# Moving rows 144 bytes from the weights in place of 64, modulo 256, in a decoder step on one Trainium2 core

## The chip, the core and the metric

The kernel runs on one core of one Trainium2 chip. The metric is device time in microseconds (us) of one execution, the median of several runs. The core has TensorE (PE: matrix products; its weight loads are listed apart as PEld), VectorE (DVE), ScalarE (ACT), GpSimd (POOL) and SyncE (SP), which issues the transfers between the large memory and the core's own memory, SBUF. SBUF has 128 partitions; a tensor in it takes the same range of bytes in each of its partitions, and this range is what "address" means below. A matrix product takes 128 x 128 weights, which a weight load brings into TensorE, and streams "moving rows" against them: 128 partitions of, for example, 288 float32 columns.

## What is computed

One step of one layer of a decoder with two kinds of head, RWKV-7 and retention, on 16 meta tokens, a prompt of 256 tokens and 8 x 4 sampled tokens (304 tokens in all), with width 2048:

```python
xn = rms_norm(x, norm_mix)
z = xn @ w_in                                   # 2048 -> 3360 + 4096 columns
o_a, S_a = rwkv7_mixer(z[..., :RWKV_COLS], ...) # 16 heads of 64
o_b, S_b = retention_mixer(z[..., RWKV_COLS:], ...)  # 4 heads of 256
h = x + concatenate([o_a, o_b]) @ w_out
hn = rms_norm(h, norm_ffn)
h = h + (silu(hn @ w_gate) * (hn @ w_up)) @ w_down   # 2048 -> 5632 -> 2048
y = rms_norm(h, norm_final)
```

Outputs are `y` without the meta tokens, the last projected row for the token shift, and both kinds of state.

## The kernel before

**Products in three passes.** All large products are float32 in value, but run as one-pass products on a rounded type (`float32r`). Each weight tile and each row is split into a high part (`wh`, `xh`) and the rest (`wl`, `xl`), and a tile product is the sum of three: `wh` x `xh`, `wh` x `xl`, `wl` x `xh` (lines 719 to 721). The small products of the mixers run on plain float32 and are not one-pass.

**The main loop** (`main`, lines 683 to 726) walks through a fixed list of weight tiles: first the input projection (`in`, 16 steps of 128 rows for each tile of 128 output columns), then the output projection in two halves of 8 steps (`out`), then the feed-forward part (`gate`, `up`, and `down` in groups of 4 steps). Weights come as 128 x 512 pieces: `wr` is filled by a transfer (`load`), ScalarE rounds it into `wh`, VectorE subtracts into `wl` (`cast` and `rest`); five buffers each.

**Columns of the moving rows.** A job says which columns of a row it streams (`cols`). Most input jobs stream all 304 (`T`). Those of the r part, and the second and third of the first three, start at column 14 (290 columns). Those of the retention gates and of q start at column 16 (288 columns). Output and feed-forward jobs work without the meta tokens and stream columns 0 to 288 (`TO`). A column is 4 bytes, so a job that starts at column 16 reads from an address 64 bytes further on than one that starts at column 0.

**Where things lie.** `xh` and `xl` are tiles of 16 rows of `XW` = 320 columns (1280 bytes, five times 256), so all 16 rows have one address modulo 256. They are the first tiles of the pool `cp`, followed by `pv`, `ones`, `omu`, `cst`, `shout` and `half`. Behind this pool lie `wr`, `wh` and `wl` (2048 bytes each), and then two arenas, one of float32 and one of float32r, in which all other tiles have places that a planner found. The down products' rows (`act`, two rows of `XW` for each tile) lie in the float32r arena; `GAP` columns at the end of the float32 arena set where that one begins.

**Order.** The order of all instructions is worked out ahead in a draft of the program, from operations and sizes, and then kept. `half` holds four sets of eight scalars for each partition, written once by four VectorE operations and read by ScalarE as bias and scale in each of the eight pairs of heads (`pair`, lines 1001 to 1010); `omu` holds scalars of the token shift.

Of the kernel before, what the change touches and what calls it, by code (L numbers as in the profile page):

```python
# [8 lines left out]
F32 = mybir.dt.float32  # L9
F32R = mybir.dt.float32r  # L10
# [5 lines left out]
P = 128  # L16
D = 2048
KT = D // P
# [4 lines left out]
T = META + SEQ + NB * NS  # L23
XW = T + 16
TO = SEQ + NB * NS
# [51 lines left out]
KEYS = ((0, META, SEQ, 0), (P, P, NP - P, SEQ), (LASTK, 2 * P, T - 2 * P, SEQ + NP - P))  # L77
RMW = SEQ + NP - P + T - 2 * P
ROOM = 33040
GAP = 56  # L80
WIDE = 4200
FREE, GAPS, TRIES = 800.0, (2000.0, 1000.0, 500.0, 200.0, 50.0, 0.0), 12

# [120 lines left out]
def pack(x_prompt, x_sample, state_shift, state_rwkv, state_ret, meta_tokens, norm_mix, w_in,  # L204
# [55 lines left out]
    r = r.reshape(NB // 2, 2, RH, 2, P, RD)  # L260
    out["s0r"] = ca(r.transpose(2, 0, 4, 3, 1, 5))
    c, rm, cs, _ = constants()
    out["cst"], out["rmask"], out["cs"] = c, rm, ca(cs)
    return out
# [34 lines left out]
class Timed:  # L299


    def __init__(self, plan, eng, name):
        self._plan, self._eng, self._name = plan, eng, name
# [280 lines left out]
class Step:  # L584


    def __init__(self, tc, I, O, ctx, rooms, draft, log):
        self.tc, self.nc, self.I, self.O = tc, tc.nc, I, O
        self.rooms, self.draft = rooms, draft
        pool = lambda n, b, **k: ctx.enter_context(tc.tile_pool(name=n, bufs=b, **k))  # L590
        self.cp = pool("const", 1)
        self.wp = pool("weights", 1)
        self.mp = pool("scratch", 1)
        self.ap_ = pool("acc", ACC, space=bass.MemoryType.PSUM)
        self.pp = pool("psum", 8 - ACC, space=bass.MemoryType.PSUM)
        self.n, self.tags = 0, {}
        self.plan = pl = Plan(self.nc, rooms, draft, log, (lambda i: i) if draft else tc.keep_in_program_order)
        self.sp = pl.sp
        if not draft:
            self.arena = {dt: self.mp.tile([P, r.size + (GAP if dt == F32 else 0)], dt, tag=f"arena_{dt}", name=f"arena_{dt}")  # L600
                          for dt, r in rooms.items()}
        self.pe, self.dve, self.act, self.pool = pl.pe, pl.dve, pl.act, pl.pool
        pl.outside = {v.name for v in (*I.values(), *O.values())}
        self.outs = []
        self.live = 0
        self.done = set()
# [182 lines left out]
    def start(self):  # L789
        I = self.I  # L790
        self.pvt = self.t([P, NPV], "pv", pool=self.cp)
        self.ones = self.t([P, P], "ones", pool=self.cp)
        self.dve.memset(self.ones, 1.0)

        self.omu = self.t([P, 46], "omu", pool=self.cp)
        self.eps = {}
        for c, e in enumerate((RMS_EPS, GN_EPS, 4 * RMS_EPS), 27):
            self.eps[e] = self.omu[:, c:c + 1]
            self.pool.memset(self.eps[e], e)
        xh, xl = self.xh, self.xl  # L800
        warm = self.t([P, 1], "warm")
        self.act.activation(warm, self.ones[:, :1], AF.Tanh)

        gx = self.t([P, KT + KT * T], "xr")
        self.gx = gx[:, :KT]
        xr = self.xr = gx[:, KT:].rearrange("p (k t) -> p k t", t=T)
        x = lambda a, b: self.sp.dma_start(xr[:, a:b], xT(I)[:, a:b, :])
        self.sp.dma_start(gx[:, :KT + T], I["xT"][:, :KT + T])
        self.load(2)
        x(1, 2)  # L810
        self.load(2)
        self.sp.dma_start(self.pvt, I["pv"])
        x(2, 3)
        self.load(2)
        x(3, 4)
        self.load(2)
        for k in range(4, KT, 2):
            self.load()
            x(k, k + 2)
        self.converted = 0  # L820

        pt = self.ps()
        for _ in range(WARM):
            self.pe.matmul(pt[:, :P], self.ones, self.ones, start=True, stop=True)
# [12 lines left out]
    def constants(self):  # L837

        I, xr = self.I, self.xr
        self.csr = self.t([P, 2, T], "csr")  # L840
        self.sp.dma_start(self.csr, I["cs"])
        self.shin = self.t([P, 27, NB], "shin")
        self.sp.dma_start(self.shin, I["shift"])
        self.cst = self.t([P, NCV], "cst", pool=self.cp)
        self.sp.dma_start(self.cst, I["cst"])
        for g in range(0, KT, 4):
            self.act.activation(xr[:, g:g + 4], xr[:, g:g + 4], AF.Square)
            if g % 8:
                self.dve.tensor_add(xr[:, g - 4:g], xr[:, g - 4:g], xr[:, g:g + 4])
            yield  # L850
        for a, n in (8, 4), (2, 2), (1, 1):
            self.dve.tensor_add(xr[:, :n], xr[:, :n], xr[:, a:a + n])
        yield
        yield
        ssq = self.ps()
        self.pe.matmul(ssq[:, :T], self.ones, xr[:, 0, :], start=True, stop=True)
        self.rstd1 = self.t([P, T], "rstd")
        yield
        yield from self.rsqrt(ssq[:, :T], 1.0 / D, RMS_EPS, out=self.rstd1)
        self.dve.tensor_mul(self.csr, self.csr, self.rstd1[:, None, :].to_broadcast([P, 2, T]))  # L860
        self.shout = self.t([P, 27, 9], "shout", pool=self.cp)
        self.pool.memset(self.shout, 0.0)

        self.half = self.t([P, 4, 8], "half", pool=self.cp)
        for i, n in enumerate(("w0", "a0", "ka")):
            self.dve.tensor_scalar(self.half[:, i, :], self.pvt[:, PV[n]:PV[n] + 8], 0.5, None, op0=ALU.mult)
        self.dve.tensor_scalar(self.half[:, 3, :], self.pvt[:, PV["ka"]:PV["ka"] + 8], -0.5, 1.0,
                               op0=ALU.mult, op1=ALU.add)
        self.dve.tensor_scalar(self.omu[:, :27], self.pvt[:, :27], -1.0, 1.0, op0=ALU.mult, op1=ALU.add)
        self.done.add("const")  # L870
# [848 lines left out]
    def ffn_jobs(self):  # L1719
        dve, act = self.dve, self.act  # L1720
        hold = {}

        def gu_post(f, f0, up, acts, last):
            def g(acc):
                t = self.t([P, TO], "fu" if up else "fg")
                dve.tensor_mul(t, acc[:, :TO], self.rstd2)
                yield
                if not up:
                    act.activation(t, t, AF.Silu)
                    hold[f] = t  # L1730
                    return
                while f not in hold:
                    yield
                dve.tensor_mul(t, t, hold.pop(f))
                yield
                hl = self.t([P, 2, XW], "act", F32R)[:, :, :TO]
                act.copy(hl[:, 0, :], t)
                yield
                dve.tensor_sub(hl[:, 1, :], t, hl[:, 0, :])
                acts[f - f0] = hl[:, 0, :], hl[:, 1, :]  # L1740
                if last:
                    self.done.add(("act", f))
            return g
# [51 lines left out]
    def build(self, gam4):  # L1795
        self.gam4 = gam4
        self.shifts = 0
        self.os, self.on, self.gates, self.ht, self.xs_of = [None] * KT, {}, {}, [], {}
        self.xh = self.t([P, KT, XW], "xh", F32R, pool=self.cp)[:, :, :T]
        self.xl = self.t([P, KT, XW], "xl", F32R, pool=self.cp)[:, :, :T]  # L1800
        self.xs = [(self.xh[:, k, :], self.xl[:, k, :]) for k in range(KT)]
        jobs = [self.z_job(i, self.lora_post(i), c0=META - 2 if i else 0) for i in range(3)]
        for h in range(NPAIR):
            jobs += self.pair_jobs(h)
        for h in range(RH):
            jobs += self.ret_jobs(h) + self.gate_jobs(h)
        jobs += self.out_jobs(0) + self.out_jobs(1) + self.ffn_jobs()
        jobs = {j.key: j for j in jobs}
        self.raws, self.halves, self.rests, self.loaded, self.halved = [], [], [], 0, 0
        self.start()  # L1810
        self.plan.run(self.main(jobs))
        self.flush(all=True)
# [5 lines left out]
def xT(I):  # L1818

    return I["xT"][:, KT:].rearrange("p (k t) -> p k t", t=T)  # L1820
# [19 lines left out]
def body(tc, I, O):  # L1840
    from contextlib import ExitStack
    gam4 = constants()[3]
    rooms = {F32: Room(), F32R: Room()}
    nc = draft(I, O)
    log = []
    Step(tile.TileContext(nc[0]).__enter__(), nc[1], nc[2], ExitStack(), rooms, True, log).build(gam4)
    rooms[F32R].place(WIDE)
    rooms[F32].place(ROOM - rooms[F32R].size)
    with ExitStack() as ctx:
        Step(tc, I, O, ctx, rooms, False, log).build(gam4)  # L1850
# [22 lines left out]
```

## Time and profile before

| what | value |
|---|---|
| median of 3 runs | 1545.88 us (1543.72 to 1546.4) |
| span of the profiled execution | 1544.2 us, the only time of it that is shown |
| busy, TensorE products | 1527.5 us, 99% of the span |
| busy, weight loads | 1499.9 us, 97% |
| busy, VectorE | 1089.4 us, 71% |
| busy, ScalarE | 866.5 us, 56% |
| mean granted clock of TensorE | 0.996 |

The profile was taken in one execution. Busy time of TensorE counts from the start of an instruction to its modelled end, and neighbouring products overlap, so the mean duration of a product (near 295 ns) is longer than the distance between two starts. Line 310 in the profile is the helper through which every instruction goes, so that groups are told apart by their operands and shapes. A product of the main loop is shown as `acc<-xh,wh`; `arena_dt.float32r` in the place of `xh` is a row of `act`.

### The profile page before, as it was taken

The numbers are of one execution on the slowest core, as the hardware profiler recorded it, in microseconds if no ns is written. First come the engines' busy times: TensorE is split into PE (matmuls) and PEld (weight loads), VectorE is DVE, ScalarE is ACT, GpSimd is POOL, SyncE is SP. The second block draws the span as 40 slices with busy tenths as digits, with TensorE's granted clock in tenths as the row PEclk, the third lists the DMA queues.
The fourth block names the chain that finished last, engine by engine and source line by source line (L and its number), as shares of the span: only waits on it lengthen the run. The fifth ranks groups of instructions, "written<-read, shape, count | busy, mean of one in ns | idle before, by whom it ended". The sixth has DMA issues, their size and how long they took to land.

```text
span 1544.2 us, 31919 instructions
## 1 busy us (share of the span) xinstructions
PE 1527.5 (99%) x11446; PEld 1499.9 (97%) x11446; DVE 1089.4 (71%) x2782; ACT 866.5 (56%) x2031; POOL 27.7 (2%) x161
## 2 busy tenths in 40 slices
PE   9999999999999999999999999999999999999997
PEld 8999999999999998999999999999999999999997
DVE  6989789899989878676656555556565656565656
ACT  6775876787876865555444444444444444444446
POOL 1000000000000000000000000000000000000000
PEclk9999999999999999999999999999999999999998
DMA  7544445434444576655555555555555555555553
GB/s 229 175 144 141 124 113 153 126 115 155 157 124 136 182 247 210 207 171 162 167 171 164 164 168 166 169 167 169 170 162 171 164 167 168 170 165 172 162 173 117
DMA packets 136334, 252.33 MB, mean 163 GB/s; under 512 B 15984, under 2 KB 22256, under 8 KB 136176
## 3 DMA queue, kind: packets, MB, share of 16 engines
q1 hardware_dynamic: 136176, 250.29, 53.5%
q8 instruction: 91, 1.49, 0.4%
q14 instruction: 67, 0.55, 0.1%
HBM read 235.95 MB, written 14.28 MB: 162 GB/s over the span
## 4 chain that ended last, share of the span: by engine, by line
PE 88%; DVE 7%; ACT 3%; issue 1%; DMA 0%; SPq 0%; DVEq 0%; ACTq 0%
PE acc L310 78%; PE mm L310 10%; DVE arena_dt.float L310 5%; ACT arena_dt.float L310 2%; DVE wl L310 2%; ACT wh L310 1%; DMA arena_dt.float<-xT 0%; SPq L310 0%; DVE arena_dt.float32r L310 0%; ACT arena_dt.float32r L310 0%; DVE xl L310 0%; ACT xh L310 0%; DVEq L1869 0%; ACT shout L310 0%; DVEq L310 0%
## 5 line engine op out<-in xcount | busy, mean ns | idle before, releaser
L310 PE MATMUL acc<-xh,wh 128*128 128x288 f32 (+2 forms) x2592 | 789.8, 305 | 2.6 <-ACT wh L310 1.8
L310 PE MATMUL acc<-xh,wl 128*128 128x288 f32 (+2 forms) x2592 | 765.5, 295 | 0.3 <-DVE wl L310 0.3
L310 PE MATMUL acc<-xl,wh 128*128 128x288 f32 (+2 forms) x2592 | 765.1, 295 | 0.1
L310 ACT CAST wh<-wr 128x512 fp32r<-128x512 f32 (+1 forms) x827 | 501.4, 616 | 350.8 <-PE acc L310 313.0
L310 DVE TENSOR_TENSOR wl<-wr,wh 128x512 fp32r<-128x512 f32 (+1 forms) x827 | 560.2, 685 | 131.0 <-ACT wh L310 128.1
L310 PEld LDWEIGHTS acc<-xh,wh 128*128 128x128 f32 x2592 | 486.2, 188 | 9.6 <-issue 3.7
L310 PEld LDWEIGHTS acc<-xl,wh 128*128 128x128 f32 x2592 | 486.0, 188 | 4.6 <-issue 1.2
L310 PEld LDWEIGHTS acc<-xh,wl 128*128 128x128 f32 x2592 | 485.3, 187 | 1.1 <-DVE wl L310 0.6
L310 PE MATMUL acc<-arena_dt.float32r,wh 128*128 128x288 f32 x1408 | 278.9, 294 | 0.4 <-ACT arena_dt.float32r L310 0.3
L310 PEld LDWEIGHTS acc<-arena_dt.float32r,wh 128*128 128x128 f32 x1408 | 224.9, 188 | 0.9 <-ACT arena_dt.float32r L310 0.6
L310 PE MATMUL acc<-arena_dt.float32r,wl 128*128 128x288 f32 x704 | 206.7, 294 | 0.0
L310 DVE TENSOR_TENSOR arena_dt.float<-acc,arena_dt.float 128x288 f32<-128x288 f32 (+4 forms) x181 | 72.7, 420 | 167.9 <-PE acc L310 167.6
L310 DVE TENSOR_TENSOR arena_dt.float<-arena_dt.float 128x288 f32<-128x288 f32 (+22 forms) x694 | 175.2, 286 | 12.0 <-ACT arena_dt.float L310 7.6
L310 ACT ACTIVATE arena_dt.float<-arena_dt.float 128x288 f32<-128x288 f32 (+7 forms) x245 | 104.6, 433 | 116.7 <-DVE arena_dt.float L310 114.8
L310 PE MATMUL mm<-arena_dt.float 128*128 128x128 f32 (+7 forms) x1136 | 167.7, 302 | 0.6 <-issue 0.2
L310 DVE TENSOR_TENSOR arena_dt.float<-arena_dt.float,acc 128x288 f32<-128x288 f32 (+1 forms) x210 | 94.4, 451 | 95.8 <-PE acc L310 95.6
L310 PEld LDWEIGHTS mm<-arena_dt.float 128*128 128x128 f32 (+1 forms) x1136 | 141.3, 181 | 11.4 <-issue 3.6
L310 PEld LDWEIGHTS acc<-arena_dt.float32r,wl 128*128 128x128 f32 x704 | 132.1, 188 | 0.0
L310 ACT COPY arena_dt.float<-mm 64x64 f32<-64x64 f32 (+11 forms) x330 | 91.4, 286 | 49.0 <-PE mm L310 44.0
L310 ACT CAST arena_dt.float32r<-arena_dt.float 128x288 fp32r<-128x288 f32 (+4 forms) x73 | 30.5, 422 | 91.1 <-DVE arena_dt.float L310 90.4
L310 ACT COPY arena_dt.float<-arena_dt.float 128x32 f32<-128x32 f32 (+7 forms) x235 | 57.1, 293 | 13.3 <-DVE arena_dt.float L310 11.5
L310 DVE SCALAR_TENSOR_TENSOR arena_dt.float<-arena_dt.float 128x288 f32<-128x288 f32 (+3 forms) x96 | 43.1, 451 | 2.3 <-ACT arena_dt.float L310 0.5
(66 smaller groups left out, 564.8 us busy)
## 6 DMA issues: line engine op xcount, KB each, us to landing
wr<-big SPq DMA_DIRECT2D x823, 256.0 KB, 2.8
arena_dt.float<-s0r SPq DMA_DIRECT2D x16, 512.0 KB, 5.2
out_rts<-arena_dt.float SPq DMA_DIRECT2D x16, 512.0 KB, 4.4
arena_dt.float<-xT SPq DMA_DIRECT2D x4, 576.0 KB, 4.7
arena_dt.float<-lora SPq DMA_DIRECT2D x16, 128.0 KB, 2.6
arena_dt.float<-s0w SPq DMA_DIRECT2D x8, 256.0 KB, 2.9
out_rws<-arena_dt.float SPq DMA_DIRECT2D x8, 256.0 KB, 3.5
out_y<-arena_dt.float SPq DMA_DIRECT2D x7, 288.0 KB, 2.4
```

Of the source, the lines that this page charges most:

```text
L310: return self._plan.keep(f(*a, **k))
```

## The change

Every moving row of the main loop's products starts 16 bytes later, and the weights lie 64 bytes lower. `LEAD` = 4 columns is left free ahead of the rows in `xh`, `xl` and `act` (the tiles stay as wide, 320 columns). `half`, 128 bytes, leaves the pool `cp`, and its scalars go behind the float32 arena, into the columns that `GAP` adds; `omu` grows from 46 to 58 columns, which takes 64 bytes more. So all that lies behind `half` is 64 bytes lower. `GAP` grows from 56 to 68 columns, which takes 64 bytes more, so that the float32r arena stays where it was, and the rows of `act` in it start 16 bytes later too. Rows that start at column 0 then lie 144 bytes from the weights modulo 256 in place of 64, those that start at column 14 200 in place of 120, those at column 16 208 in place of 128.

```diff
-GAP = 56
+GAP = 68
+LEAD = 4
...
             self.arena = {dt: self.mp.tile([P, r.size + (GAP if dt == F32 else 0)], dt, tag=f"arena_{dt}", name=f"arena_{dt}")
                           for dt, r in rooms.items()}
+            o = rooms[F32].size
+            self.spare = self.arena[F32][:, o:o + 32].rearrange("p (a b) -> p a b", b=8)
...
-        self.omu = self.t([P, 46], "omu", pool=self.cp)
+        self.omu = self.t([P, 58], "omu", pool=self.cp)
...
-        self.half = self.t([P, 4, 8], "half", pool=self.cp)
+        self.half = self.t([P, 4, 8], "half", pool=self.cp) if self.draft else self.spare
...
-                hl = self.t([P, 2, XW], "act", F32R)[:, :, :TO]
+                hl = self.t([P, 2, XW], "act", F32R)[:, :, LEAD:LEAD + TO]
...
-        self.xh = self.t([P, KT, XW], "xh", F32R, pool=self.cp)[:, :, :T]
-        self.xl = self.t([P, KT, XW], "xl", F32R, pool=self.cp)[:, :, :T]
+        self.xh = self.t([P, KT, XW], "xh", F32R, pool=self.cp)[:, :, LEAD:LEAD + T]
+        self.xl = self.t([P, KT, XW], "xl", F32R, pool=self.cp)[:, :, LEAD:LEAD + T]
```

## The prediction

> **What bounds the kernel now.** I read the page first (share of each engine, the 40 slices, the chain that ended last), then who waited for whom on TensorE, then the groups of products by shape, then the timeline for the pace of the products.
>
> ```profile
> span 1544.2 us, 31919 instructions
> PE 1527.5 (99%) x11446; PEld 1499.9 (97%) x11446; DVE 1089.4 (71%) x2782; ACT 866.5 (56%) x2031; POOL 27.7 (2%) x161
> PEclk9999999999999999999999999999999999999998
> PE 88%; DVE 7%; ACT 3%; issue 1%; DMA 0%; SPq 0%; DVEq 0%; ACTq 0%
> PE acc L310 78%; PE mm L310 10%; DVE arena_dt.float L310 5%; ACT arena_dt.float L310 2%; DVE wl L310 2%; ACT wh L310 1%; DMA arena_dt.float<-xT 0%; SPq L310 0%; DVE arena_dt.float32r L310 0%; ACT arena_dt.float32r L310 0%; DVE xl L310 0%; ACT xh L310 0%; DVEq L1869 0%; ACT shout L310 0%; DVEq L310 0%
> ```
>
> TensorE is busy for 99% of the span at the full granted clock, and 88% of the chain lies on it, 78% on the products that write `acc`. The waits agree: the longest one of TensorE on another engine is 1.8 us.
>
> ```profile
> PE acc L310 <- ACT wh L310: 1.8, 1, 1.8
> ```
>
> So the time is the number of products times the distance from one start to the next. A product's busy time in the page (near 295 ns) is not that distance, because products overlap; the distance has to be read from starts. Here is one long stretch of the feed-forward part, with nothing but one-pass products of 288 columns, and the busy time of all engines beside it.
>
> ```profile
> core 0: us, PE busy (x) PEld busy (x) DVE busy (x) ACT busy (x) POOL busy (x), PEclk, DMA share, GB/s
> 720.00:1500.00 780.00, 780.00 (x5927) 780.00 (x5926) 459.09 (x821) 330.06 (x578) 0.00 (x0) 1.00 0.56 167
> 660.00:700.00 40.00, 40.00 (x306) 40.00 (x305) 30.66 (x61) 24.07 (x50) 0.00 (x0) 1.00 0.55 159
> 1200.00:1240.00 40.00, 40.00 (x306) 40.00 (x305) 25.00 (x48) 16.83 (x29) 0.00 (x0) 1.00 0.55 163
> ```
>
> Of the 5927 products two began before 720.00, so 5925 starts in 780 us: **131.65 ns** each. The two short stretches hold 306 products each although VectorE is busy for 30.66 us in one and 25.00 us in the other. The pace therefore doesn't depend on what VectorE and ScalarE do beside it. It is TensorE's own.
>
> **The change part by part.** It adds and removes no instruction. The four VectorE operations that fill `half` stay, the casts and subtractions that write the rows stay, and every DMA stays with its size. What moves is where things lie (all distances between rows and weights here are modulo 256 bytes, as in the change's own words). Rows of `xh`, `xl` and the `act` tiles start 16 bytes later, `wr`, `wh` and `wl` lie 64 bytes lower, `half` moves behind the float arena, `omu` takes 64 bytes more. The order of the instructions is drawn up from sizes and not from addresses, so it stays too.
>
> First the parts that I cost at nothing. Writers and readers of moved tiles run on VectorE (71%) and ScalarE (56%). If a write to a row that begins 16 bytes later were slower, the cover is TensorE's 99%; without that cover it would show in the waits on `wh`, `wl` and `xh`, now 1.8 us at most. The 823 loads of `wr` land 64 bytes lower; the chain has DMA at 0%.
>
> That leaves the products. They are 9936, by shape:
>
> ```profile
> L310 PE MATMUL acc<-xh,wh 128*128 128x288 f32 x1920 | 572.1, 298 | 0.8 <-ACT xh L310 0.8
> L310 PE MATMUL acc<-arena_dt.float32r,wh 128*128 128x288 f32 x1408 | 278.9, 294 | 0.4 <-ACT arena_dt.float32r L310 0.3
> L310 PE MATMUL acc<-arena_dt.float32r,wl 128*128 128x288 f32 x704 | 206.7, 294 | 0.0
> L310 PE MATMUL acc<-xh,wh 128*128 128x304 f32 x512 | 168.0, 328 | 0.0
> L310 PE MATMUL acc<-xh,wh 128*128 128x290 f32 x144 | 44.5, 309 | 0.0
> L310 PE MATMUL acc<-xh,wh 128*32 128x290 f32 x16 | 5.2, 323 | 1.8 <-ACT wh L310 1.8
> L310 PE MATMUL mm<-xh,wh 128*128 128x304 f32 x16 | 5.3, 334 | 0.6 <-ACT wh L310 0.6
> ```
>
> Each row on `xh,wh` has two of equal count beside it (`xl,wh` and `xh,wl`). 288 columns: 3 x 1920 + 1408 + 704 = 7872. 304 columns: 3 x (512 + 16) = 1584. 290 columns: 3 x (144 + 16) = 480.
>
> Does the place of the rows matter at all? The trace of before has rows at three places, since a job that leaves out the first columns starts further on in the same row. Full rows (304 columns) and the rows of the output and feed-forward products (288) start 64 bytes from the weights. The input products of the gates and of q start at column 16 (288 columns): 64 more bytes, **128**. The r products and two of the first three start at column 14 (290 columns): 56 more, **120**. Here are the first and the last row of one unbroken stretch of each: 41 products of 288 columns at 128, then 48 of 290 at 120, then 104 of 304 at 64, each to the start of the next.
>
> ```profile
> 227.10 0.29 PE L310 MATMUL acc<-xh,wh 128*128 128x288 f32 x1
> 227.10 0.19 PEld L310 LDWEIGHTS acc<-xl,wh 128*128 128x128 f32 x1
> ...
> 232.57 0.29 PE L310 MATMUL acc<-xh,wl 128*128 128x288 f32 x1
> ```
>
> ```profile
> 96.30 0.30 PE L310 MATMUL acc<-xh,wh 128*128 128x290 f32 x1
> ...
> 102.71 0.30 PE L310 MATMUL acc<-xh,wh 128*128 128x304 f32 x1
> ```
>
> ```profile
> 127.82 0.30 PE L310 MATMUL acc<-xh,wh 128*128 128x304 f32 x1
> ...
> 142.16 0.30 PE L310 MATMUL acc<-xh,wl 128*128 128x304 f32 x1
> ```
>
> - 288 columns at 128: 5.47 us / 41 = 133.4 ns, against 131.65 ns at 64 with the same columns: **1.75 ns more**.
> - 304 columns at 64: 14.34 us / 104 = 137.9 ns. That is 6.25 ns over 288 columns at 64, or 0.39 ns a column.
> - 290 columns at 120: 6.41 us / 48 = 133.5 ns. Two columns more than 288 would give 131.65 + 0.78 = 132.4 ns, so 120 costs 1.1 ns more than 64.
>
> The second row of the first stretch shows the likely reason: the load of the next weights begins in the same 10 ns as the product, so both read memory side by side, and their distance decides how they meet. That is an inference; the three paces are measured.
>
> No row lies at 144. From below, the bound is that 144 is as much better than 64 as 128 is worse, -1.75 ns. From above, I carry the climb on: 1.75 ns over the 64 bytes from 64 to 128 is 0.44 ns in 16 bytes, so +2.2 ns at 144. I take the nearest row, 128, which is 16 bytes away: **+1.75 ns**.
>
> - 288 columns that go from 64 to 144: all but those of the gates and q. These are 16 tiles (two for each of four heads, twice) of 16 steps and 3 products, 768; 7872 - 768 = 7104. 7104 x 1.75 ns = 12.4 us.
> - 304 columns, from 64 to 144: 1584 x 1.75 ns = 2.8 us.
> - Gates and q go from 128 to 208, the 480 of 290 columns from 120 to 200. No long stretch shows such places; between the ends of plus and minus 1248 x 1.75 ns = 2.2 us I take 0.
>
> Sum: **+15.2 us**, none of it hidden, since each product starts behind the one before. On the profiled span 1544.2 + 15.2 = 1559.4 us. The median of the runs shown, 1545.88 us, is 1.7 us over that span, so the timed kernel should come to **1561 us**. What is late next stays TensorE: a slower pace gives the others more room.
>
> Now the rule that speaks against any effect. The Trainium skill, "TensorE: Matmul & The Clock Gate", in its step-by-step section, says that TensorE reads moving rows and weights through two independent ports, and that loading the next weights takes no read bandwidth from the running product. By it the sum would be 0. The trace disagrees as far as the rows go: equal products, 131.65 ns at one place and 133.4 ns at another. It stays as part of the second rival, because a difference between 64 and 144 need not follow from one between 64 and 128.
>
> **The rivals.** *Faster: 144 lies past a narrow peak, in a gap that is better than 64.* Its place is the same 8688 products. For it: from 64 to 120, in 56 bytes, the price rises by 1.1 ns, and from 120 to 128, in 8 bytes, by 0.65 ns. A price that climbs so steeply at 128 may be near its top there and be gone 16 bytes on. Also, 131.65 ns need not be the floor: at 0.39 ns a column, 288 columns account for 112 ns, and the other 19 ns are overhead, some of which may be of this kind. Against it: no row shows any place better than 64. Price: the mirror of what 128 costs, 8688 x -1.75 ns = -15.2 us, so 1529 us span and **1531 us** timed. It decides from a pace of 131.3 ns in the feed-forward part downwards, because 0.2% of the time (3.1 us) over 8688 products is 0.36 ns.
>
> *No difference: 144 meets the weights as 64 does*, on the falling side of that same peak, or the layout is not what it says. For it: the two-sided bound above has zero inside. Against it: both places measured away from 64 cost more. Time: 1546 us, within 3.
>
> **How the numbers follow.** Slower as worked out 0.44, faster 0.38, no difference 0.18. The nearest row speaks for slower, the steep climb keeps faster close behind it. Taking 0.2% as the least that a measurement of this kernel tells from no change, these are also the chances of slower, faster and same. The forecast's own range is 1551 to 1568 us: above, 8688 x 2.2 ns = 19.1 us plus the 2.2 us of the unknown places, 1567; below, a third of the price. Cases of both signs hold most of the chance, so the whole range reaches over both: from 1524 us (the faster rival with 0.75 ns more a product, 8688 x 2.5 ns = 21.7 us) to 1568 us.
>
> **What would show it.** Right: 720 to 1500 us holds about 5849 products (133.4 ns) in place of 5927, stretches of 304 columns run near 139.7 ns, counts and order of instructions are the same, and waits on `wh` and `wl` stay under 5 us. Wrong: a stretch at or under 131.7 ns, or a slower time with an unchanged pace, which would put the cost in waits, in VectorE or in ScalarE instead. Gates and q show by themselves what 208 does, r what 200 does.

## The result and the profile after

The changed kernel takes 1541.34 us (median of 9 runs, 1540.92 to 1543.2) against 1545.48 us before (9 runs): a ratio of 0.9979, with a 95% interval of 0.9969 to 0.9989. It is 0.21% faster. Forecast were 1561 us and slower.

The page of the kernel after, its span, first busy line and the chain by engine:

```profile
span 1539.1 us, 31917 instructions
PE 1523.7 (99%) x11446; PEld 1497.5 (97%) x11446; DVE 1088.6 (71%) x2782; ACT 866.8 (56%) x2031; POOL 27.7 (2%) x161
PE 96%; DVE 2%; ACT 1%; DMA 0%; issue 0%; SPq 0%; DVEq 0%; ACTq 0%
```

Nothing but the pace has moved: the counts of products, VectorE and ScalarE operations are the same, and the two instructions fewer are waits of ScalarE that went with `half`. So the answer must lie in the distance between the starts of products, called the pace below. The windows view (columns: stretch, its length, then busy time and count of each engine) of before:

```profile
620.00:700.00 80.00, 80.00 (x610) 80.00 (x609) 57.25 (x113) 44.69 (x91) 0.00 (x0) 1.00 0.58 182
```

and of after:

```profile
720.00:1500.00 780.00, 780.00 (x5952) 780.00 (x5951) 460.73 (x824) 331.40 (x579) 0.00 (x0) 1.00 0.57 168
620.00:700.00 80.00, 80.00 (x618) 80.00 (x617) 58.05 (x115) 44.78 (x91) 0.00 (x0) 1.00 0.59 184
```

From 720 to 1500 us after starts 5950 products (two began earlier) where before started 5925: 131.1 ns each against 131.65. From 620 to 700 us, mostly the output projection, it starts 616 against 608: 130 ns against 131.6. Shape and place are the same in both stretches of after, 288 columns at 144 bytes, and yet they have **two paces**. The forecast had 133.4 ns for both.

The timeline of after, first and last row of unbroken stretches: 104 products of 304 columns (now at 144), 47 of 290 (now at 200), 41 of 288 of the gates and q (now at 208):

```profile
127.30 0.30 PE L311 MATMUL acc<-xh,wh 128*128 128x304 f32 x1
...
141.85 0.30 PE L311 MATMUL acc<-xh,wl 128*128 128x304 f32 x1
```

```profile
95.50 0.30 PE L311 MATMUL acc<-xh,wh 128*128 128x290 f32 x1
...
101.92 0.30 PE L311 MATMUL acc<-xh,wl 128*128 128x290 f32 x1
```

```profile
227.28 0.29 PE L311 MATMUL acc<-xh,wh 128*128 128x288 f32 x1
...
232.74 0.30 PE L311 MATMUL acc<-xh,wl 128*128 128x288 f32 x1
```

That is 14.55 us / 104 = 139.9 ns (before 137.9), 6.42 / 47 = 136.6 ns (before 133.5) and 5.46 / 41 = 133.2 ns (before 133.4). So the change makes full input rows and the r rows slower, by 2.0 and 3.1 ns, and wins only on 288 columns in the later part.

Where the span's difference comes from, as the sum of all distances from one start to the next, by the shape of the first product, after less before:

| products | us |
|---|---|
| 288 columns, output and feed-forward | -5.1 |
| 288 columns, gates and q | -0.3 |
| 304 columns | +1.7 |
| 290 columns | -0.4 |
| all small products | -0.7 |
| sum, to the start of the last product | -4.8 |

The 290 columns don't fit their slower pace. The reason lies in the first 20 us, in the granted clock (the column behind TensorE's count), here of before, after, and a third profile of after:

```profile
5.00:20.00 15.00, 12.21 (x73) 0.89 0.97 318
```

```profile
5.00:20.00 15.00, 12.78 (x85) 1.00 0.93 319
```

```profile
5.00:20.00 15.00, 12.65 (x71) 0.89 0.94 318
```

In some executions the granted clock drops there for a few microseconds (0.89 on average over these 15 us). The profile of before is one of these, that of after is not. The third profile of after, with the drop, is 1.9 us behind the first one by the 1200th product and stays so. About 1.9 us of the 5.1 us between the spans is therefore this drop and not the change. The same sum for the third profile against before, both with the drop, is -2.9 us: -5.1 for the output and feed-forward products, +2.4 for 304 columns, +0.8 for 290, the rest -1.0. Like compared with like, the change is worth some 3 us, 0.19%. The nine times of after fall in two groups as far apart, 1540.9 to 1541.3 and 1542.8 to 1543.2 us.

### The profile page after: what moved, and what is told of

Its sections match the earlier page's. It is cut to its first block, busy times and chain, and to the rows that moved or that the text cites. A ratio compares the mean times of both kernels' runs of the same rounds, so it can differ in the third digit from the quotient of the medians.

```text
span 1539.1 us, 31917 instructions
## 1 busy us (share of the span) xinstructions
PE 1523.7 (99%) x11446; PEld 1497.5 (97%) x11446; DVE 1088.6 (71%) x2782; ACT 866.8 (56%) x2031; POOL 27.7 (2%) x161
## 4 chain that ended last, share of the span: by engine, by line
PE 96%; DVE 2%; ACT 1%; DMA 0%; issue 0%; SPq 0%; DVEq 0%; ACTq 0%
PE acc L311 84%; PE mm L311 12%; DVE arena_dt.float L311 1%; DMA arena_dt.float<-xT 0%; DVE wl L311 0%; SPq L311 0%; ACT arena_dt.float L311 0%; ACT arena_dt.float32r L311 0%; DVE arena_dt.float32r L311 0%; ACT wh L311 0%; DVE xl L311 0%; ACT xh L311 0%; DVEq L1872 0%; ACT shout L311 0%; DVEq L311 0%
## 5 line engine op out<-in xcount | busy, mean ns | idle before, releaser
L311 ACT ACTIVATE arena_dt.float<-arena_dt.float 128x288 f32<-128x288 f32 (+7 forms) x253 | 109.4, 440 | 115.8 <-DVE arena_dt.float L311 114.0
L311 PEld LDWEIGHTS mm<-arena_dt.float 128*128 128x128 f32 (+1 forms) x1136 | 141.7, 181 | 10.3 <-issue 3.3
L311 PEld LDWEIGHTS acc<-arena_dt.float32r,wl 128*128 128x128 f32 x704 | 132.2, 188 | 0.0
```

The lines of the kernel that those rows point to most:

```text
L311: return self._plan.keep(f(*a, **k))
```

## The experiments

Theory D said that the pace follows from the distance of rows and weights modulo 256, as the prediction had it. Its rivals: the rows' own address (R), the weights' own address (W), the moved `half` with its two waits.

**The two parts of the change, each alone.** The first is the kernel after with

```diff
-LEAD = 4
+LEAD = 0
```

> One part of the change: half moved, omu and GAP as in after, so the weights lie 64 bytes lower, but the rows start where they did before. Distances 128 (full rows), 184 (r), 192 (gates and q). Theory D, pace by distance: the feed-forward products go at 133.3 ns, as the gates did in the trace of before, so 7104 x 1.65 = +11.7 us for these and a time of 1555 to 1560 us. Theory R, pace by the address of the rows: 131.7 ns and 1545 us, as before. Theory half: the time comes from two ScalarE waits that are gone with half, not from the places: 1541 us as after.

Measured: 1556.76 us, ratio 1.0081 (1.0066 to 1.0096). The windows view:

```profile
720.00:1500.00 780.00, 780.00 (x5852) 780.00 (x5852) 454.66 (x812) 326.90 (x570) 0.00 (x0) 1.00 0.57 165
```

5850 products in 780 us, 133.3 ns, with rows that haven't moved. R is out, since the weights' place alone costs 12 us. `half` is out too, for it moved here as well and the time rose. The 133.4 ns that the prediction read from the gates at 128 bytes was right for 128 bytes.

The second is the kernel before with

```diff
+LEAD = 4
...
-                hl = self.t([P, 2, XW], "act", F32R)[:, :, :TO]
+                hl = self.t([P, 2, XW], "act", F32R)[:, :, LEAD:LEAD + TO]
...
-        self.xh = self.t([P, KT, XW], "xh", F32R, pool=self.cp)[:, :, :T]
-        self.xl = self.t([P, KT, XW], "xl", F32R, pool=self.cp)[:, :, :T]
+        self.xh = self.t([P, KT, XW], "xh", F32R, pool=self.cp)[:, :, LEAD:LEAD + T]
+        self.xl = self.t([P, KT, XW], "xl", F32R, pool=self.cp)[:, :, LEAD:LEAD + T]
```

> The other part: rows 16 bytes later, weights, half, omu and GAP as before. Distances 80 (full rows), 136 (r), 144 (gates and q). Theory D: the feed-forward pace is that of 80 bytes, which no trace so far shows, between 130 and 134 ns, so 1533 to 1562 us; gates and q (288 columns at 144) go at 130.0 or 131.1 ns in place of 133.3. Theory R, by the address of the rows: feed-forward at 130.0 or 131.1 ns, gates and q at 133.3 ns as in after, 1541 us. Theory half: 1545 us as before.

Measured: 1540.25 us, ratio 0.9975 (0.9966 to 0.9985). The weights need not have moved: 16 bytes on the rows alone give as much as the whole change. The windows view shows 5950 products, 131.1 ns, at 80 bytes:

```profile
720.00:1500.00 780.00, 780.00 (x5952) 780.00 (x5951) 460.78 (x824) 332.14 (x579) 0.00 (x0) 1.00 0.57 168
```

W is out too: the weights lie where they did, and the pace went from 131.7 to 131.1 ns. The gates and q, now at 144 bytes, ran at 130.0 ns in four of the five stretches of 26 products and more and at 131.1 ns in the fifth; shorter stretches show both. The rest of the input projection had other paces too: the r products at 136 bytes ran at 131.6 ns, full rows of 304 columns at 136.6 ns in some stretches and 140.0 ns in others. R had the gates at 133.3 ns, as in after, and fails here too.

**Maps of places.** In the first scan, made from the kernel before, the gate and up products read their weights from another column by turns:

```diff
...
+            q = o
+            if key[0] in ("gate", "up"):
...
+                w = 4 * (key[1] % 16)
+                q = o + w if o < 384 or w == 0 else o + w - 64
...
-            self.pe.matmul(acc[:m, :n], hi[:, o:o + m], xh, start=k == 0, stop=False)
...
+            self.pe.matmul(acc[:m, :n], hi[:, q:q + m], xh, start=k == 0, stop=False)
...
```

> The gate and up products read their weights w floats further on (w = 0, 4, ... 60 by turns, one place for the 96 products of each pair), so these 4224 products multiply the wrong weight columns; rows stay where they were in the kernel before, so the distance of rows from weights takes all 16 places in steps of 16 bytes. Theory D, the pace follows from the distance modulo 256: w=0 (64 bytes) 131.7 ns, w=48 (128 bytes) 133.3 ns, w=44 (144 bytes) 130.0 or 131.1 ns, as in the traces of before and after; other places between 127 and 136 ns. Theory R, the pace follows from the address of the rows alone: 131.7 ns at all 16 places. Theory W, the pace follows from the address of the weights alone: differs by w as under D; the next run tells them apart.

> As the run before, but the gate and up products also read their rows from column 4 on, 16 bytes later, so they also stream the wrong columns. Theory D: the same table by distance, so shifted by one step of w: w=4 (64 bytes) 131.7 ns, w=52 (128 bytes) 133.3 ns, w=48 (144 bytes) 130.0 or 131.1 ns. Theory R: one pace at all 16 places, that of after's rows at 144 modulo 256 (130.0 or 131.1 ns). Theory W: the table of the run before, unshifted by w: w=48 133.3 ns, w=0 131.7 ns.

> As the first scan, but the gate and up products stream 304 columns (16 of them left over from the input projection), so 16 more columns of work and wrong weight columns in 4224 products. If the distance alone sets an extra that is the same for every length, the table is that of 288 columns plus 6.2 ns at every place: 137.9 ns at 64 bytes, 139.5 at 128, 136.2 to 137.3 at 144. If length and distance act together, the order of the places differs from that at 288 columns: 137.8 ns at 64 and 139.9 ns at 144, as the traces of before and after have it.

Measured, as ns from start to start over each stretch of 96 products without its first eight (two or three stretches a place; where these differ, both). The row for 64 bytes in the second column holds the down products too, which stay at 64; "rows at" gives the address of the rows modulo 256:

| bytes from the weights | 288, rows at 128 | 288, rows at 144 | 304, rows at 128 |
|---|---|---|---|
| 0 | 131.7 | 131.1 | 137.8 |
| 16 | 131.7 | 131.7 | 138.3 |
| 32 | 133.3 | 133.3 | 140.0 |
| 48 | 132.3, 133.3 | 130.0 | 137.4 |
| 64 | 131.7, 132.2 | 133.3 | 137.8 |
| 80 | 132.7 | 131.1 | 140.0 |
| 96 | 131.7 | 131.1 | 141.7 |
| 112 | 131.1 | 134.8 | 140.0 |
| 128 | 133.3 | 133.3 | 140.0 |
| 144 | 132.3 | 130.0 | 140.0 |
| 160 | 133.3 | 133.4 | 140.0 |
| 176 | 131.1 | 131.4 | 140.0 |
| 192 | 133.4 | 132.3 | 138.7 |
| 208 | 131.1 | 133.3 | 140.0 |
| 224 | 133.3 | 131.7 | 140.0 |
| 240 | 132.0 | 132.0 | 140.0 |

How the table is read from the timeline, in the first scan at 208 and then at 192 bytes, 95 products each:

```profile
1115.23 0.30 PE L310 MATMUL acc<-xh,wh 128*128 128x288 f32 x1
...
1127.71 0.29 PE L310 MATMUL acc<-xh,wl 128*128 128x288 f32 x1
1127.84 0.30 PE L310 MATMUL acc<-xh,wh 128*128 128x288 f32 x1
...
1140.51 0.29 PE L310 MATMUL acc<-xh,wl 128*128 128x288 f32 x1
```

12.48 us / 95 = 131.4 ns (131.1 without the first eight), and right behind it 12.67 us / 95 = 133.4 ns. Every theory fails in part. Under D the second and third column would be alike; they differ at most places (at 112 by 3.7 ns). Under R each column would hold one value. Under W the third would be the second, moved down by one place. And length acts together with place: with rows at 128, 96 bytes is among the better places for 288 columns (131.7 ns) and the worst for 304 (141.7 ns). A limit of these maps: the products right ahead of a place are at the same other place nearly every time, so a second pace could be missed.

> As the first scan, but the gate and up products stream 290 columns from column 14 on, as the r products do, with wrong weight columns in 4224 products; distances 120 minus 16 for each step of w. If the distance alone sets an extra that is the same for every length, the price is that of the first scan's places plus 0.8 ns. If length and distance act together: 133.3 ns at 120 and 136.5 ns at 200 bytes, as the traces of before and after have it, in an order of its own.

Measured: 133.3 to 133.4 ns at 10 of the 16 places, 133.2 to 133.3 at 120; 131.1 at 24, 134.0 to 134.2 at 88, 135.0 at 168, 136.7 at 200 and 216. The change put these products at one of the two worst places.

The next one takes the step down to 4 bytes, rows alone:

```diff
...
+            if key[0] in ("gate", "up"):
+                c0 = key[1] % 17
+                c1 = c0 + n
...
```

> As rows_only, but the gate and up products read their rows from column 0 to 16 by turns, so they stream the wrong columns (4224 products); distances 80 to 144 in steps of 4 bytes, weights fixed. If the price is smooth in the distance, as the prediction had it, neighbours 4 bytes apart differ by less than 0.3 ns and the paces climb or fall steadily between 131.1 ns at 80 and 130.0 ns at 144. If it isn't smooth, neighbours jump by 1 ns and more between the same few values (130.0, 131.1, 131.7, 133.3 ns).

Measured, from 80 bytes on in steps of 4: 131.1, 136.6, 133.3, 130.0, 131.7, 136.7, 133.3, 133.3 (once 131.1), 134.6, 133.3, 136.3, 131.4, 133.3, 133.4, 136.0, 133.3, and at 144 bytes 130.0, once 131.1. From 80 to 84 bytes the pace rises by 5.5 ns; from 88 to 92 it falls by 3.3. The first stretch at 84, 12.98 us for 95 products:

```profile
706.43 0.30 PE L311 MATMUL acc<-xh,wh 128*128 128x288 f32 x1
...
719.41 0.30 PE L311 MATMUL acc<-xh,wl 128*128 128x288 f32 x1
```

The prediction's smooth price is out. The paces keep coming back to the same values, 133.3 ns above all, and none of these scans found less than 130.0 ns at 288 columns.

**Does anything of D hold?** Rows and weights both 64 bytes on, from the kernel before:

```diff
-GAP = 56
+GAP = 40
+LEAD = 16
...
-        self.omu = self.t([P, 46], "omu", pool=self.cp)
+        self.omu = self.t([P, 62], "omu", pool=self.cp)
...
```

The rows start at `LEAD` in `xh`, `xl` and `act`, as in the change.

> Rows and weights both 64 bytes further on than before, distances unchanged: 64, 120 and 128. If the distance decides as long as both move by 64 bytes, all paces of before come back: 131.7 ns (or 132.2, the other steady pace seen at that place) in the feed-forward part, 137.8 ns for 304 columns, 133.3 ns for the gates and for r, 1542 to 1549 us. If the addresses modulo 256 of each decide, other paces among 130.0, 131.1, 131.7 and 133.3 ns, 1533 to 1558 us.

Measured: 1544.78 us, ratio 1.0002 (0.9993 to 1.0011). In long stretches 131.7 or 132.2 ns (288), 137.8 (304), 133.3 (gates) and 133.3 ns (r): all the paces of before. The long stretch:

```profile
720.00:1500.00 780.00, 780.00 (x5926) 780.00 (x5925) 460.69 (x823) 331.00 (x578) 0.00 (x0) 1.00 0.56 167
```

A joint move by 64 bytes brings back the same paces and the same time; only the stretch from 609 us took 132.2 ns where before had 131.7. The maps hold smaller joint moves. By 32 bytes the paces are the same again: at 96 bytes 131.7 ns with rows at 128 and at 160, at 112 bytes 134.8 and 134.6 to 134.8 ns with rows at 144 and at 176. By 64 bytes the gates of `weights_only` at 192 bytes (133.3 ns, rows at 192) and those of after at 208 (133.3 ns, rows at 208) agree with the maps (133.4 ns, rows at 128, and 133.3 ns, rows at 144). By 16 bytes they often are others: with rows at 128 and at 144, 131.7 and 131.1 ns at 96 bytes, 131.1 and 134.8 ns at 112. So of D this much holds at the places tried: the distance decides as long as both move by a multiple of 32 bytes. Where a place has more than one pace, this is said of the set of them.

**Two paces at one place.** After ran at 130.0 ns in the output projection and at 131.1 ns in the feed-forward part, at one place. Two more profiles of the same kernel:

> The kernel after, unchanged, profiled once more, since its nine times fall into two groups (1540.9 to 1541.3 and 1542.8 to 1543.2 us) and its trace had 130.0 ns in one feed-forward stretch and 131.1 ns in the long one at the same place. If the program alone settles which of the two steady paces a stretch takes: 131.1 ns from 705 to 1501 us again. If small differences between executions settle it: sometimes 130.0 ns there, which would be 6076 x 1.1 = 6.7 us less.

> The kernel after, unchanged, a third profile: as for the second, 131.1 ns in the long stretch if the program alone settles the pace, 130.0 ns in some executions if it doesn't.

Measured: 1541.17 and 1542.84 us; in both 130.0 ns in the 682 products from about 612 us, and 131.1 ns in all 6076 products of the long stretch, as in the first. So in these two stretches the same program takes the same pace each time. It doesn't everywhere: the products behind 1502 us began near 131.2 ns in the first profile and at 130.0 ns in the other two. To see whether the way into a stretch picks its pace, after got a small product ahead of each group of down products:

```diff
+                if key[0] == "down" and key[2] == 0:
+                    self.bridge(1)
```

> The kernel after, with one small float32 product of ones by ones ahead of each of the eleven groups of down products, its result unused. Theory, one place one pace: the feed-forward stretches go on at 131.1 ns, and eleven interruptions of about 0.2 us make it 2 to 3 us slower than after, 1543 to 1545 us. Rival, the way into a stretch picks one of several steady paces: stretches at 130.0 and at 131.1 ns side by side in one execution, 1536 to 1545 us.

Measured: 1537.82 us, ratio 0.9958 (0.9941 to 0.9974), faster than after with eleven products more (span 1535.2 us against 1539.1). The windows view, ahead of the first added product, behind it, and far later:

```profile
706.00:756.00 50.00, 50.00 (x384) 50.00 (x383) 28.73 (x50) 23.70 (x42) 0.00 (x0) 1.00 0.55 168
762.00:812.00 50.00, 50.00 (x387) 50.00 (x386) 30.59 (x56) 21.02 (x36) 0.00 (x0) 1.00 0.57 169
1210.00:1260.00 50.00, 50.00 (x387) 50.00 (x386) 30.61 (x57) 20.88 (x37) 0.00 (x0) 1.00 0.58 169
```

The 403 products ahead of the first interruption go at 131.1 ns, and all ten long stretches behind an interruption at 130.0 ns, with the other engines and the transfers about as busy. One place has more than one steady pace, and in after the long stretch kept its own for 796 us.

That the way in picks it, the first scan shows without any added product. Its down products all lie at 64 bytes, but the gate and up products right ahead of them lie at one of four places by turns. Behind 0 bytes they ran at 131.7 ns, in three stretches of three; behind 192 bytes at 132.2 ns, in three of three. The first stretch of each, 191 products in 25.15 us and in 25.25 us:

```profile
759.85 0.29 PE L310 MATMUL acc<-arena_dt.float32r,wh 128*128 128x288 f32 x1
...
785.00 0.29 PE L310 MATMUL acc<-arena_dt.float32r,wl 128*128 128x288 f32 x1
```

```profile
836.01 0.30 PE L310 MATMUL acc<-arena_dt.float32r,wh 128*128 128x288 f32 x1
...
861.26 0.29 PE L310 MATMUL acc<-arena_dt.float32r,wl 128*128 128x288 f32 x1
```

There is no pause between the two kinds of products; the change of place is enough.

**A version that beats both.** In `rows_only` the gates showed 130.0 ns at 144 bytes with rows at 208 modulo 256. So: input rows as there (16 bytes later), rows of the output and feed-forward products at column 20 (80 bytes later), weights where they were. The edit, against `rows_only`, in its main lines:

```diff
+LATER = 20
...
-                hl = self.t([P, 2, XW], "act", F32R)[:, :, LEAD:LEAD + TO]
+                hl = self.t([P, 2, XW], "act", F32R)[:, :, LATER:LATER + TO]
...
+        self.yh, self.yl = xh[:, :, LATER:LATER + TO], xl[:, :, LATER:LATER + TO]
...
```

> Weights, half and omu as before; the input projection's rows 16 bytes later (as in rows_only), the rows of the output and feed-forward products 80 bytes later than before, so that they have the place that the gates and q have in rows_only (144 bytes from the weights, rows at 208 modulo 256), where these went at 130.0 ns. Theory, the pace belongs to the pair of places and the length: 130.0 ns in the feed-forward part too, 1.1 ns less than in rows_only, 7104 x 1.1 = 7.8 us, so about 1532 us. Rival, a place has several steady paces and the way into a stretch picks one: 131.1 ns or another in part of it, 1532 to 1540 us.

Measured: 1533.33 us, ratio 0.9927 (0.9913 to 0.9942). The windows view:

```profile
720.00:1480.00 760.00, 760.00 (x5849) 760.00 (x5848) 453.43 (x811) 326.42 (x570) 0.00 (x0) 1.00 0.56 169
620.00:690.00 70.00, 70.00 (x537) 70.00 (x536) 49.16 (x95) 36.85 (x74) 0.00 (x0) 1.00 0.62 190
```

5847 products in 760 us are 130.0 ns; from 620 to 690 us, 535 are 130.8, and from start to start of the unbroken stretch there 131.1. Here the long stretch took up the faster pace and the shorter one the slower, the reverse of after.

## Why the prediction was wrong, step by step

- **What bounds the kernel: right.** TensorE's pace alone moved the time. VectorE, ScalarE and transfers kept their shares, and the edits costed at nothing cost nothing that can be seen: `weights_only` moved `half` too and got the time that its products' pace gives.
- **The three paces of before: right as read, their cause half right.** At 128 bytes in place of 64 the same products take 1.7 ns more: `weights_only` put all 7104 there and lost 0.81%. So rows and weights act together, as the inference had it. That "their distance decides" doesn't hold alone: at 112 bytes the maps have 131.1 and 134.8 ns.
- **"I take the nearest row, 128, which is 16 bytes away": this step failed.** It put 288 columns at 144 bytes at 133.4 ns; they ran at 131.1 and 130.0 ns. For the 7104 products it gave +12.4 us, and they brought -5.1 us. The scans show why: the price is not smooth in the distance, steps of 4 bytes move it by up to 5.5 ns, so the price at 128 couldn't stand for the one at 144. The bound from above, 2.2 ns by carrying the climb on, was drawn from the same wrong picture; it held for 144 bytes by luck.
- **304 columns, +2.8 us: right in size by accident.** At 144 bytes they cost 2.0 ns more (forecast 1.75), about +2.5 us over the 1300 or so with another right behind them; in the sums they come to +1.7 us, and to +2.4 us with the clock drop on both sides. But they did so while 288 columns at the same place became faster. One price for both lengths was the second error of that step. The 0.39 ns a column, read at 64 bytes, isn't general either: at 144 the same 16 columns take 8.9 or 10.0 ns more than 288 do, 0.56 or 0.63 ns a column.
- **"I take 0" for the places 200 and 208: half right.** Gates and q kept 133.2 ns at 208. The r products at 200 lost 3.1 ns, above the bound of 1.75; over 480 that would be 1.5 us. The sums have -0.4 us, with the clock drop in before alone, and +0.8 us with it on both sides.
- **The faster rival had the sign and not the size.** It held 144 to be a better place than 64 because the climb at 128 was steep; irregular is what the scans show, and the gain on 288 columns was 0.55 ns in the long stretch. In the output projection it was 1.7 ns, near the 1.75 of this rival, but full rows lost 2.0. The remark that 131.65 ns need not be the floor was borne out (130.0).
- **The rule of two independent ports** (the Trainium skill, "TensorE: Matmul & The Clock Gate", step-by-step section), by which the sum would be 0, doesn't fit `weights_only`: the weights' place alone moved the pace from 131.7 to 133.3 ns, with the same rows and columns. The rival of no difference is out as well: 64 and 144 bytes gave different paces at both lengths.
- **What the prediction didn't have at all:** that a place can have two paces. With 130.0 ns in the long stretch too, 6076 x 1.1 ns = 6.7 us less, after would have come near 1535 us.

Open: what in the reading of rows and weights makes these paces. The runs show that both places and the length enter, and that joint moves by 32 and 64 bytes, where there were any, don't. The mechanism wasn't tried. Open too is what it is in the products on the way in that picks a pace, and the paces of 304 columns with rows at other addresses than those here.

## What to carry to other kernels

Where back-to-back products bound a kernel, the pace is worth measuring at each place that is considered, for each length, with distances between starts: a scan of all places fits in one run when the products of each tile read from another column. Each place in it shows the pace that its own way in picked, so the place chosen has to be timed in the kernel itself. Don't interpolate between places, and expect that what is saved at one length may be paid back at another. Give each stage its own place where the row has spare columns, and look at every long stretch for a second, slower pace that a small interruption can shake off.

## What the runs showed of the hardware that I had not expected

- The distance from start to start at 288 columns in long stretches took five values, 130.0, 131.1, 131.7, 132.2 and 133.3 ns, whatever VectorE and ScalarE did; the short stretches of the maps add others, up to 136.7 ns.
- Places 4 bytes apart differ by up to 5.5 ns a product (131.1 at 80 bytes, 136.6 at 84).
- At one place two steady paces stand side by side (130.0 and 131.1 ns at 144 bytes; 136.6 and 140.0 ns for 304 columns at 80), and one of them lasted for 6076 products. At 64 bytes the place of the products just ahead picked between 131.7 and 132.2 ns.
- A drop of the granted clock in the first 20 us (0.89 on average over 15 us), in some executions and not in others: of one kernel, the execution with it was 1.9 us behind one without.
